# RG-LRU of a two-layer diffusion backbone: channel blocks as a pipeline skewed by one block and split by direction, without barriers, the residual kept in SBUF between post-norm and pre-norm

## Chip, cores, metric

One Trainium2 chip, 8 cores, one batch element per core (batch 8). The metric is the device time of the slowest core in microseconds (us). Cores 0 to 3 are one die, 4 to 7 the other.

Executions come in two states. In the slow one the cores of one die, or of both, show a lower granted TensorE clock and the time is some per cent longer, whatever the kernel. Ratios are the mean time of one kernel's fast runs over that of the other's of the same rounds, so not quite the ratio of the medians.

## The reference, cut to what matters

```python
D_MODEL = 2048; BATCH = 8; SEQ = 2048; CTX_LEN = 256; LRU_BLOCK = 128; D_FF = 5632; DEPTH = 2

def rglru_coeffs(v, wa, ba, wx, bx, lam):
    r = jax.nn.sigmoid(block_diag(v, wa, ba));  i = jax.nn.sigmoid(block_diag(v, wx, bx))
    log_a = -RG_C * r * jax.nn.softplus(-lam)
    return jnp.exp(log_a), jnp.sqrt(-jnp.expm1(2.0 * log_a)) * i * v

# layer 0
x   = ffn_sublayer(x, ..., w_in[0, 0], w_out[0, 0])       # pre-norm, SwiGLU, post-norm, gated residual
ctx = ffn_sublayer(ctx, ...)                              # same weights, other modulation
hx, hc = modulate(rmsnorm(x)), modulate(rmsnorm(ctx))
g, v  = jnp.split(hx @ w_in, 2, axis=-1)
v     = centred_dwconv(v)                                 # 4 taps inside each row of 64 tokens
v_ctx = centred_dwconv(hc @ w_in[:, R:])
for d, reverse in enumerate((False, True)):
    h_c  = linear_scan(*rglru_coeffs(v_ctx, ...), 0, reverse)
    y   += linear_scan(*rglru_coeffs(v, ...), h_end_of(h_c), reverse)
x = x + gate * rmsnorm((gelu(g) * y) @ rec_w_out)
x = ffn_sublayer(x, ..., w_in[0, 1], w_out[0, 1])
# layer 1: FFN, Fourier mixer, FFN.  Every shift, scale and gate is an adaLN product silu(c) @ mod_w + b
```

## The kernel before: the parts that matter

A helper records every operation with what it reads and writes, and lets the issuing engine wait for whatever is outstanding on those. A tile is tracked as a whole, not by columns:

```python
def _deps(self, stream, reads, writes):
    for r in reads:
        self._wait(stream, r.w)
    for w in writes:
        self._wait(stream, w.w)          # the last write of the same tile
        for ev in w.r:
            self._wait(stream, ev)       # its readers
```

adaLN products run in the background of the first FFN's gate/up phases; VectorE empties their PSUM:

```python
def adaln_task(l, idx, W):               # a 1 MB load, 32 matmuls of 2 columns, one evacuation
    ...
    S.op("pe", pe, reads=[rb, r_scb], writes=spair_res(k))
    S.op("dve", evac, reads=spair_res(k) + [r_vecs], writes=[r_mods[l][idx // 2]])
ada = [adaln_task(0, i, W) for i in range(32, 144, 2)]               # 56 of them
gu_phase(W, 0, 0, T0[0], stat_steps(T0[1], 0), ada[:20])             # ada[20:40], ada[40:] in the next two
```

The RG-LRU starts with the last tile's post-norm and pre-norm through memory and a barrier, and handles one block of 128 channels after the other:

```python
def rglru(carry, hx, hcb):
    for st in carry:                     # 32 post-norm and pre-norm chunks: load, compute, store, load again
        st()
    S.barrier()
    ... # weights of blocks 0 and 1, projections and convolution of block 0
    for c in range(KC):                  # 16 blocks
        ... # PE: context gates of both directions -> ACT: tanh, exp
        for d in range(2):               # PE: 8 gate matmuls, ACT: 4 tanh, 1 exp
            ...
        emit_v(c + 1)                    # PE: recurrent projection of the next block
        ... # DVE: squares; ACT: sqrt; DVE: products
        stage1(c + 1)                    # PE: gate projection; ACT: copy, gelu; DVE: convolution
        ... # DVE: four scans (context and tokens, two directions), sum, times gelu -> zs in HBM
    S.barrier()
... # zs is read back, then the output projection (mix_out), tile 0 and tile 1
```

## Time and profile before

Runs of before: 10679.41, 11927.26, 10470.75 us, and a profiled one of 10495.78 (fast). The stages below are read from the trace, as means over its 8 cores.

| stage | us |
|---|---|
| up to the end of the first FFN (three tiles, gate/up and down projections) | 2447 |
| of which gate/up of the middle tile | 572 |
| lead-in: last FFN matmul to first gate matmul of block 0 | 257 |
| 15 block periods (57.4 each) | 862 |
| tail: last block and output projection of tile 0 | 200 |
| output projection of tile 1 | 286 |
| the rest (second FFN, layer 1) | 6423 |
| all | 10476 |

The page's rows by slice of 262 us, here the DMA share (tenths) and GB/s, show why the stages have different limits:

```profile
DMA  9988878985211278986997687566555566565545
GB/s 166 155 144 162 166 143 162 180 166 139 42 30 31 51 191 170 172 157 128 166 176 142 135 169 161 118 128 125 107 133 154 152 149 122 105 131 122 122 90 140
```

The first FFN keeps the DMA engines at seven to nine tenths. In the RG-LRU, slices 11 to 14, they fall to one or two: there is room for the adaLN weights.

### The profile page before, as it was taken

What the parts mean: (1) busy time and instruction counts of PE and PEld (TensorE: products, weight loads), DVE (VectorE), ACT (ScalarE), POOL (GpSimd) and SP (SyncE); (2) the same over time, 40 slices, a digit from 0 to 9 for tenths busy, and PEclk for the clock granted to TensorE, in tenths of its full rate; (3) what the DMA queues carried; (4) which work ended last, traced back from release to release, by engine and by line L of the source; (5) the groups of instructions that cost most, each with busy time, mean ns of one, the idle gap of its engine ahead of it and who ended that gap; (6) DMA issues with size and microseconds to landing.
All of it is one profiled execution on the core that took longest, in us unless ns stands there. A gap on an engine that the chain in (4) does not pass through costs nothing.

```text
span 10494.4 us, 126561 instructions; the slowest of 8 cores (10445.1 to 10494.4 us)
## 1 busy us (share of the span) xinstructions
PE 8912.0 (85%) x47328; PEld 4369.6 (42%) x47967; DVE 2776.5 (26%) x3790; ACT 1943.4 (19%) x3068; POOL 534.5 (5%) x935
## 2 busy tenths in 40 slices
PE   3998899993567567999999999999984479999995
PEld 2655555652223223444444444444432134444442
DVE  1112211223577632121221133112224322111102
ACT  1111111122454322111111111111113221110000
POOL 0000000000000000000000000000000000000000
PEclk9999999996777688999999999999996789999997
DMA  9988878985211278986997687566555566565545
GB/s 166 155 144 162 166 143 162 180 166 139 42 30 31 51 191 170 172 157 128 166 176 142 135 169 161 118 128 125 107 133 154 152 149 122 105 131 122 122 90 140
DMA packets 541141, 1416.33 MB, mean 135 GB/s; under 512 B 65400, under 2 KB 215032, under 8 KB 489600
## 3 DMA queue, kind: packets, MB, share of 16 engines
q0 software_dynamic: 153888, 830.83, 48.1%
q1 hardware_dynamic: 386656, 577.37, 19.4%
q8 instruction: 395, 6.47, 0.3%
q14 instruction: 202, 1.65, 0.1%
HBM read 1995.21 MB, written 222.30 MB: 211 GB/s over the span
## 4 chain that ended last, share of the span: by engine, by line
PE 78%; DMA 12%; ACT 3%; DVE 3%; issue 3%; SPq 1%; DVEq 0%; ACTq 0%; POOL 0%; POOLq 0%; another core or an unknown queue 0%
PE PS L170 50%; PE PS L569 25%; DMA xl_17_67<-xT 1%; DMA xl_20_70<-xT 1%; DMA w_30_80<-modw 1%; DMA xl_20_70<-xs 1%; PE PS L325 1%; DMA xl_21_71<-xs 1%; DMA xl_19_69<-xT 1%; DMA xl_16_66<-xs 1%; PE PS L756 1%; PE PS L369 1%; PE PS L759 1%; DMA xl_15_65<-xT 0%; DMA xl_21_71<-xT 0%
## 5 line engine op out<-in xcount | busy, mean ns | idle before, releaser
L384 DVE TENSOR_TENSOR acc_12_62<-acc_12_62,sq_25_75 128x512 f32<-128x512 f32 (+1 forms) x150 | 97.8, 652 | 2027.4 <-ACT sq_25_75 L383 1955.2
L170 PE MATMUL PS<-hb_29254,w_69_29251 128*128 128x512 bf16 x2381 | 527.6, 379 | 3.4 <-ACT acc_12_62 L373 0.7
L170 PE MATMUL PS<-hb_29254,w_67_29249 128*128 128x512 bf16 x2314 | 514.5, 379 | 2.8
L170 PE MATMUL PS<-hb_29254,w_70_29252 128*128 128x512 bf16 x2119 | 474.6, 380 | 9.3 <-DMA w_70_29252<-win 6.3
L170 PE MATMUL PS<-hb_29254,w_68_29250 128*128 128x512 bf16 x2119 | 471.8, 379 | 4.3 <-DVE hid_29253 L546 1.0
L170 PE MATMUL PS<-hb_29254,w_66_29248 128*128 128x512 bf16 x2064 | 459.7, 380 | 3.2 <-issue 0.5
L170 PE MATMUL PS<-hb_82,w_28_78 128*128 128x384 bf16 x2240 | 376.4, 329 | 56.7 <-ACT hb_82 L449 36.4
L170 PE MATMUL PS<-hb_82,w_30_80 128*128 128x384 bf16 x2240 | 374.3, 328 | 20.8 <-DVE mods_2_44 L332 13.9
L170 PE MATMUL PS<-hb_82,w_29_79 128*128 128x384 bf16 x2240 | 373.4, 328 | 12.1 <-DVE mods_2_44 L332 12.0
L170 PEld LDWEIGHTS PS<-hb_29254,w_69_29251 128*128 128x128 bf16 x2432 | 236.7, 98 | 283.8 <-issue 0.6
L170 PEld LDWEIGHTS PS<-hb_29254,w_67_29249 128*128 128x128 bf16 x2368 | 230.5, 98 | 277.0 <-issue 1.8
L170 PEld LDWEIGHTS PS<-hb_29254,w_70_29252 128*128 128x128 bf16 x2176 | 212.5, 98 | 262.2 <-issue 9.7
L170 PEld LDWEIGHTS PS<-hb_29254,w_68_29250 128*128 128x128 bf16 x2176 | 212.4, 98 | 257.2 <-issue 4.7
L170 PEld LDWEIGHTS PS<-hb_29254,w_66_29248 128*128 128x128 bf16 x2112 | 206.0, 98 | 247.4 <-issue 3.4
L170 PEld LDWEIGHTS PS<-hb_82,w_28_78 128*128 128x128 bf16 x2240 | 219.3, 99 | 204.3 <-issue 64.8
L544 ACT ACTIVATE ev_23_73<-PS 128x512 f32<-128x512 f32 (+1 forms) x264 | 147.5, 559 | 834.2 <-PE PS L170 774.9
L544 ACT ACTIVATE ev_24_74<-PS 128x512 f32<-128x512 f32 (+1 forms) x266 | 148.6, 559 | 821.8 <-PE PS L170 767.7
L170 PE MATMUL PS<-hb_82,w_27_77 128*128 128x384 bf16 x1728 | 286.9, 327 | 14.1 <-DVE mods_2_44 L332 13.2
L544 ACT ACTIVATE ev_22_72<-PS 128x512 f32<-128x512 f32 (+1 forms) x262 | 145.9, 557 | 821.9 <-PE PS L170 788.1
L170 PEld LDWEIGHTS PS<-hb_82,w_30_80 128*128 128x128 bf16 x2240 | 219.4, 98 | 168.1 <-issue 26.7
L170 PEld LDWEIGHTS PS<-hb_82,w_29_79 128*128 128x128 bf16 x2240 | 219.3, 98 | 158.9 <-issue 17.1
L569 PE MATMUL PS<-hid_29253,w_67_29249 128*128 128x512 bf16 x1122 | 251.3, 381 | 5.3 <-DVE hid_29253 L546 2.1
(638 smaller groups left out, 12563.4 us busy)
## 6 DMA issues: line engine op xcount, KB each, us to landing
w_69_29251<-win POOLq DMA_DIRECT2D x38, 1024.0 KB, 13.7
w_67_29249<-win POOLq DMA_DIRECT2D x37, 1024.0 KB, 13.4
w_28_78<-win POOLq DMA_DIRECT2D x35, 1024.0 KB, 13.8
w_29_79<-win POOLq DMA_DIRECT2D x35, 1024.0 KB, 14.1
w_30_80<-win POOLq DMA_DIRECT2D x35, 1024.0 KB, 14.0
w_68_29250<-win POOLq DMA_DIRECT2D x34, 1024.0 KB, 12.1
w_70_29252<-win POOLq DMA_DIRECT2D x34, 1024.0 KB, 12.3
w_66_29248<-win POOLq DMA_DIRECT2D x33, 1024.0 KB, 12.7
```

What stands on the lines that cost most here:

```text
L170: ins = e.matmul(out, l, r, start=(i == 0), stop=(i == n - 1))
L325: ins = e.matmul(o, w, scb[:, 2 * c:2 * c + 2], start=(c == 0), stop=(c == KC - 1))
L369: ins = e.matmul(sbank(k, h, n), ones[:], acc[:, h * n:(h + 1) * n], start=True, stop=True)
L384: S.op("dve", lambda e: e.tensor_tensor(out=a, in0=a, in1=sb[:, :n], op=ALU.add), reads=[rsq], writes=[r_acc])
L544: S.op("act", lambda e, tb=tb, h=h, k=ks[0]: e.activation(out=tb[:, :n], in_=sbank(k, h, n), func=AF.Silu), reads=[rPS[2 * ks[0] + h]], wr ...
L569: ins = e.matmul(sbank(k, h, n), buf[:, (c - a) * 128:(c - a + 1) * 128], rhs(c, h), start=(c == 0), stop=(c == nk - 1))
L756: e.matmul(bank(PB, t2), gwa, vcb[:, lo + t2 * TT:lo + (t2 + 1) * TT], start=True, stop=True)
L759: ins = e.matmul(bank(PB, 2 + t2), gwx, vcb[:, lo + t2 * TT:lo + (t2 + 1) * TT], start=True, stop=True)
```

## The change

Its intent: (1) let TensorE work on the next block's projections between the gates of this one, one direction after the other, so that gates, exponentials, scans and projections overlap; (2) no barrier before or after the recurrence, and no reload of the last block; (3) keep the last tile's residual in SBUF from post-norm to pre-norm; (4) move 32 of 56 adaLN tasks from the first FFN into the idle DMA time of the recurrence.

```diff
-    ada = [adaln_task(0, i, W) for i in range(32, 144, 2)]
+    ada = [adaln_task(0, i, W) for i in range(32, 80, 2)]
-    gu_phase(W, 0, 0, T0[0], stat_steps(T0[1], 0), ada[:20])          # then [20:40], [40:]
+    gu_phase(W, 0, 0, T0[0], stat_steps(T0[1], 0), ada[:10])          # then [10:17], [17:]
-    rglru(post_steps(T0[2], 0, 1, 0, 0) + pre_steps(T0m[2], 1, 0, 1, mdst, r_mdst), hx, hcb)
+    W, posts = rglru(W, T0[2], hx, hcb, r_hxs, TS)

+    def post_resident(tl, l, s, ro, xr, r_xr, yr, slot):              # lead-in, 16 chunks of 768 columns
+        def load(m):
+            S.dma("sp", dn, ... out=yb, in_=ys[...])
+            for (off, w, src, dst, t0, which) in segs:                # 512 latent, 256 context columns
+                S.dma("sp", f"xr{m}", ... out=xr[m][:, off:off + w] ..., writes=[r_xr[m]])
+        for m in range(yr.n - 1): load(m)
+        rstd(acc, r_acc, n, slot=slot)
+        for m in range(KC):
+            ...                                                       # DVE: y * rstd, x += gate * y
+            S.op("act", ... AF.Square ...)
+            S.dma("act", f"xw{m}", ...)                               # store x, which also stays in xr[m]
+            S.op("pe", stat, ...)                                     # sum of squares
+        rstd(rsx[ro], r_rsx[ro], n, slot)

+        for b in range(3): proj(0, 0, b)                              # block 0, five banks, ahead of the above
+        for b in range(2): proj(0, 1, b)
+        post_resident(tl, 0, 0, 1, xr, r_xr, yr, 3)

+        for c in range(KC):                                           # vch, gch: chunks of block c + 1
+            g0[0](); g0[1](); hsum()                                  # hsum on POOL (sum of directions)
+            for i in range(3): take(vch); g0[2 + i]()
+            take(vch); expo(c, 0); pmul(c, 0); conv(nx, 0); msqrt(); zout(c - 1)
+            take(vch); take(vch)
+            g1[0](); take(vch); g1[1](); take(vch); g1[2](); take(gch); g1[3](); take(gch); g1[4]()
+            scan(c, 0); take(gch)
+            i0 = ada_pe(0); ada_pe(1); expo(c, 1); pmul(c, 1)         # expo(c, 1): its square on POOL
+            take(gch); conv(nx, 1); ctx_proj(nx); ctx_conv(nx); cast(nx)
+            ada_pe(2); msqrt(); take(gch); take(gch); ada_pe(3); take(gch); take(gch)
+            ada_evac(i0); scan(c, 1); gelu(nx)
... # tail: the last block's product goes straight into the matmul operand; no barrier, no reload
```

## The prediction

> **What bounds the kernel now.** I began with the page, then cut the span by the chain that ended last and asked for the busy time of each stretch. Columns: stretch, its length, then TensorE (PE), its weight loads, VectorE (DVE), ScalarE (ACT), GpSimd (POOL) busy with instruction counts; last the granted PE clock, the DMA share, GB/s.
>
> ```profile
> PEclk9999999996777688999999999999996789999997
> ...
> 203.00:684.00 481.00, 476.67 (x3431) 292.49 (x3430) 69.96 (x142) 55.91 (x124) 36.92 (x63) 1.00 0.91 148
> 920.00:1504.00 584.00, 495.11 (x3468) 298.08 (x3468) 132.29 (x237) 78.11 (x161) 37.47 (x64) 0.92 0.87 160
> 1741.00:2220.00 479.00, 476.65 (x3339) 291.12 (x3340) 112.17 (x204) 61.67 (x126) 34.56 (x60) 0.99 0.95 173
> 2456.00:2712.00 256.00, 37.77 (x151) 17.20 (x155) 98.66 (x161) 53.58 (x90) 3.75 (x6) 0.58 0.43 109
> 2712.00:3582.00 870.00, 611.18 (x2419) 261.92 (x2461) 625.52 (x418) 421.83 (x396) 16.26 (x26) 0.77 0.13 28
> 3582.00:3667.00 85.00, 7.24 (x15) 1.74 (x16) 38.25 (x21) 19.20 (x17) 2.65 (x5) 0.50 0.42 98
> 3667.00:3773.00 106.00, 105.26 (x475) 47.73 (x485) 18.01 (x26) 29.35 (x57) 7.49 (x15) 0.99 0.77 174
> 3773.00:4063.00 290.00, 138.52 (x575) 59.55 (x583) 122.89 (x162) 82.91 (x139) 10.07 (x18) 0.74 0.79 194
> ```
>
> The first three rows are the gate/up phases of the three tiles of the first FFN; the middle one is 103 us longer, at about the same PE work. 2456 to 2712 is the lead-in of the RG-LRU: last post-norm, last pre-norm, barrier, block 0's projections; PE works 38 of 256 us. 2712 to 3582 is 15 steady blocks of 58.0 us, where no engine is full: PE 41 us, DVE 42, ACT 28 each. After 3582 comes the last block with a barrier and a reload of z (85 us), then the output projection of tile 0 (106) and of tile 1 (290, held by transfers).
>
> Two lists of waits name the holders, for PE from 920 to 1220 and from 2456 to 2712 (total, times, longest):
>
> ```profile
> PE PS L170 <- DVE mods_2_44 L332: 52.9, 5, 13.9
> ...
> PE PS L369 <- DVE rsx_14_64 L384: 133.5, 1, 133.5
> PE PS L170 <- DMA wi_35_24157<-recin: 77.4, 1, 77.4
> ```
>
> Line 332 empties an adaLN product out of PSUM. It sits on DVE behind post-norm steps that wait for x loads, and PE runs out of PSUM slots. Then 133.5 us is PE waiting while 32 small post-norm chunks go through memory; the 77.4 us that look like a weight load are really the pre-norm chunks ahead of the barrier.
>
> These rows from the whole kernel and from one block's time order (start, us) price the operations:
>
> ```profile
> L806 DVE TENSOR_TENSOR_SCAN bH_49_24171<-bC_47_24169,cH_24186,bB_45_24167 128x2048 f32<-128x2048 f32 x16 | 71.7, 4484 | 1.7
> L775 DVE TENSOR_TENSOR bH_48_24170<-bC_46_24168 128x2048 f32<-128x2048 f32 x16 | 36.7, 2292 | 114.5 <-ACT bC_46_24168 L769 114.5
> L763 ACT ACTIVATE bA_24165<-PS,hgb_24187 128x1024 f32<-128x1024 f32 x64 | 71.3, 1114 | 96.2 <-PE PS L759 96.2
> ...
> 2963.34 15.77 PE L170 MATMUL PS<-hx_20830,wi_36_24158 128*128 128x512 bf16 x63
> 2967.76 1.28 ACT L778 ACT_TABLE_LOAD   x1
> 2969.47 1.99 ACT L780 ACTIVATE bH_48_24170<-bH_48_24170,oneb_51 128x2048 f32<-128x2048 f32 x1
> 2981.24 13.97 PE L170 MATMUL PS<-hx_20830,wi_36_24158 128*128 128x512 bf16 x63 [2.13 <-ACT vp_24162 L693]
> ```
>
> A warm 512-column matmul costs 14/64 = 0.219 us start to start, so eight (half a bank) cost 1.75.
>
> **The Trainium skill.** (1) "GPSIMD Engine Reference", Elementwise side-by-side cycle accounting: a 2048-column fp32 two-input op takes 4497 ns on GpSimd, 2293 on VectorE. The 2292 above agrees; GpSimd computes nothing in this trace, so I scale: 5.1 us for 2304 columns, an estimate. (2) "SBUF — State Buffer", Who interferes with whom: a VectorE op with two SBUF inputs and a GpSimd op that reads SBUF exclude each other. No run yet shows it. (3) "ScalarE: Activation LUTs", What ACT_TABLE_LOAD costs: 1283 ns plus a drain of about 1380. The trace agrees with the load and shows no drain: load at 2967.76, next activation at 2969.05. (4) "TensorE: Matmul & The Clock Gate", Part 1: an idle window of about 3.4 us halves the clock. The two 63-matmul runs agree: 15.77 after the thinly used gate stage, 13.97 after a 2.1 us gap, so 1.8 us a cold start.
>
> **Part 1, adaLN moved out of the first FFN.** 32 of its 56 double tasks go to the RG-LRU as 64 single ones; the three phases keep 10, 7, 7 of 20, 20, 16. One task is 0.78 us of PE (chain) and a 1 MB load. Tiles 0 and 2, full of PE, save 10 and 9 tasks: 8 + 7 us. Tile 1 saves 13 x 0.78 = 10 us and most of its 584 - 495 = 89 us idle, because 13 of the 64 weight-sized loads go and line 332 with them: I take 80. Sum 105.
>
> **Part 2, lead-in.** Post-norm now runs on 16 chunks of 768 columns with six loads ahead, x stays in SBUF, squares are summed by PE, and pre-norm rereads nothing. PE does five banks of projections meanwhile (80 x 0.219 = 17.5 us, hidden). Loads 16 x 2 x 393 KB = 12.6 MB, stores 6.3 MB; at the 194 to 200 GB/s of the output stretch, 95 us for all. Allow 90 until the last chunk; square sum, square root and the 5.0 us reciprocal 10; pre-norm 16 x 1 us (ACT: 0.56 + 0.42) 16; remaining projections, convolution and casts 16. Sum 132 against 256: saves 124.
>
> **Part 3, the block.** Context and tokens become one 2304-column scan per direction, convolutions read PSUM, one square and the sum of directions go to GpSimd. Work per block: PE 128 x 0.219 + gates 4 + context 1.9 + adaLN 1.6 = 35.5; DVE: conv 7.6, context 1.6, casts 1.7, two products of 2.56 per direction 10.2, scans 10.1, output 2.3 = 33.5; ACT: tanh 10.8, exp 6.9, sqrt 4.4, identity 2.5, gelu 2.2, five table loads 6.4 = 33. Nobody alone would take 36, but the gates share one PSUM pair (banks 6, 7) while PE runs in order. Walk from PE's last projection chunk at 0: gelu of its half 1.4; table load and two context tanh 3.6; four gate tanh, each one chunk plus two gate matmuls (2.2) apart, end at 12.2; two exp 16.8; identity, table load and sqrt 21.3; table load and context tanh 23.6. PE ran out at 18.1, waiting for that tanh to free bank 6. From there: gates to 30.8, then chunk, adaLN, chunk, context projection, adaLN, four chunks: 44.9. I add 2 for the third adaLN weight, whose buffer is refilled only after the first is used (half of the 8.2 us of a 1 MB block load), and 2 for a cold start. Period 49, saving 15 x 9 = 135. DVE ends its second scan at about 51, which overlaps the next block's gates.
>
> **Part 4, tail.** No barrier; the last block ends at about 55 (GpSimd sum after the last scan, direct product into the matmul operand) with three output columns accumulated up to 14/16 in the shadow; then 13 x 32 x 0.219 + 3 = 94. 149 against 85 + 106 = 191, less 5 for evacuation: saves 38. Tile 1's projection keeps its small chunks and its 50 MB (six streams of 8.4) at 194 GB/s: still about 290.
>
> Sum 105 + 124 + 135 + 38 = 402. The fast executions of before are 10471 and 10496, mean 10483; so 10080 in the fast state. The other two, 10679 and 11927, are slower in a way that I put down to the chip's slow state.
>
> **Rivals.** (a) *The recurrence stays bound by the ACT–PE ping-pong through banks 6 and 7.* With cold starts at both stalls, slow GpSimd and a sixth table load the period is 54 and the loop saves 60: total about 325, 10160. For it: the clock of 0.77 in the loop, and that all engines need 33 to 36. Against: seven chunks fill the gate gaps, as nothing did before. (b) *The true pipeline works* and the period is 41 to 43: saves 240, total 505, 9980. It would need ACT to get through exp, sqrt and two loads before PE runs out; the walk says 5 us late. (c) *The lead-in is hidden badly*: if small-row transfers give only 110 GB/s, as 2456 to 2712 averaged, its loads and stores take 170 and it saves 40. Against: that stretch is latency with two or three loads ahead, not bandwidth. (d) *The DMA relief of tile 1 does not come*, because 66 norm steps in 42 ticks still wait for loads: saves 40 instead of 90. All of a, c and d at their worst still leave about 190 us, just under 2%.
>
> **Range and chances.** Independent errors of 40 (loop), 30 (lead-in), 30 (FFN), 15 (tail) give about 60; 8 in 10 is 80 on the fast side, widened upwards for the slow state: 9980 to 10220. The 2% line is 10275: faster 0.90, same 0.09, slower 0.01.
>
> **What would show it.** Right: the middle gate/up phase under 510 us with PE full; under 150 us from the end of the first FFN to the first tanh; block period 47 to 52 with one PE gap of 5 to 7 us in front of the second direction's gates, put down to ACT; GpSimd products of about 5 us; no gap for z at the end. Wrong: a period over 55 or under 43; DVE products stretched to 5 us or more beside GpSimd's (the port); later phases longer because the output projection's transfers moved.

## The result, and the profile after

The changed kernel's four timed runs were 10169.65 and 10143.57 (fast), 11012.23 and 11619.86 (slow): median 10590.94. A fifth run took 10156.6 (fast). The trace read below is that of the run of 10169.65. Those of before, in the same rounds, were 10470.75 and 10464.84 (fast), 10679.41 and 11927.26: median 10575.08. The medians mix states and say nothing of the change. The ratio of the fast runs is 0.9703, with a 95% interval of 0.9672 to 0.9733: 3.0% faster.

Stages, in us, mean of the 8 cores of each profiled run; the lower rows are the experiments, told below (e3_store_late and e9_best: only the four cores of the undisturbed die). The metric, the time of the slowest core, moves less in places: the means of the fast runs are 10156.6 for the changed kernel and 10138.9, 10206.2, 10153.4 (one run), 10111.0, 10069.9, 10126.2, 10033.8, 10028.8 and 9991.1 (one run) for e1 to e9. Fast runs of one kernel differ by up to 27 us, so effects smaller than that are read from the stages and not from the totals.

| kernel | first FFN | of it middle gate/up | lead-in | 15 blocks | period | tail | tile 1 | rest | all |
|---|---|---|---|---|---|---|---|---|---|
| before | 2447 | 572.5 | 256.9 | 861.6 | 57.4 | 200.3 | 286.0 | 6423 | 10476 |
| changed | 2359 | 506.2 | 148.8 | 769.2 | 51.3 | 156.5 | 285.5 | 6429 | 10148 |
| difference | -88 | -66 | -108 | -92 | -6.1 | -44 | 0 | +5 | -328 |
| predicted | -105 | -90 | -124 | -135 | -9 | -38 | 0 | 0 | -402 |
| e1_ada_late | 2365 | 509.0 | 147.0 | 720.5 | 48.0 | 157.3 | 286.8 | 6426 | 10102 |
| e2_ada_back | 2461 | 580.0 | 147.6 | 713.8 | 47.6 | 151.6 | 286.7 | 6421 | 10183 |
| e3_store_late | 2359 | 504.4 | 131.7 | 768.8 | 51.3 | 156.7 | 289.4 | 6413 | 10118 |
| e4_chunks_early | 2364 | 510.8 | 148.6 | 697.5 | 46.5 | 159.7 | 289.4 | 6422 | 10081 |
| e5_both | 2364 | 509.4 | 130.7 | 697.2 | 46.5 | 158.8 | 286.3 | 6417 | 10054 |
| e6_one_wait | 2362 | 506.9 | 116.5 | 767.4 | 51.2 | 157.6 | 287.6 | 6416 | 10107 |
| e7_lead | 2361 | 506.7 | 98.1 | 697.2 | 46.5 | 159.4 | 286.5 | 6418 | 10020 |
| e9_best | 2328 | 471.6 | 100.8 | 681.4 | 45.4 | 161.0 | 287.9 | 6426 | 9985 |

The page of the changed kernel, granted clock by slice, answers to the first line that the prediction shows:

```profile
PEclk9999999997898879999999999999977799999997
```

The hollow of the clock around the recurrence is shorter and less deep. The stretches, with the same columns as in the prediction: three gate/up phases, lead-in, 15 blocks, tail, tile 1.

```profile
200.60:670.90 470.30, 468.88 (x3108) 284.20 (x3108) 67.64 (x129) 57.07 (x125) 29.22 (x52) 0.99 0.73 129
911.50:1417.60 506.10, 476.35 (x3055) 285.89 (x3054) 132.58 (x226) 77.74 (x163) 28.10 (x51) 0.97 0.84 156
1658.00:2126.00 468.00, 465.20 (x3010) 281.17 (x3008) 110.10 (x190) 59.79 (x125) 27.07 (x50) 1.00 0.85 155
2360.30:2511.40 151.10, 45.81 (x186) 17.73 (x184) 70.14 (x84) 44.58 (x63) 2.11 (x4) 0.62 0.56 143
2511.40:3281.00 769.60, 597.97 (x3418) 272.55 (x3417) 489.82 (x316) 494.67 (x405) 172.50 (x118) 0.90 0.38 72
```

TensorE is busy for 598 of 770 us in the blocks, 78% instead of 70%, and the granted clock there rises from 0.77 to 0.90. The middle gate/up phase still has about 30 us without TensorE work. The list of TensorE's waits in it (who waited, for what, total, times, longest) names the same holder as before, smaller:

```profile
PE PS L178 <- DVE mods_2_44 L356: 22.7, 2, 11.8
```

Line 356 is line 332 of before, the evacuation of an adaLN product: 55.6 us in 6 waits became 22.7 in 2.

Lines of one block in the order of time (start, us, engine, line; in brackets the idle time before it and what ended it). The prediction's walk puts its zero at the end of the last projection chunk, here 2974.3:

```profile
2983.73 1.12 ACT L855 ACTIVATE gB_47_21849<-PS,hgb_56 128x1024 f32<-128x1024 f32 x1 [1.04 <-PE PS L851]
...
2990.78 1.19 ACT L778 ACTIVATE vcA_21845<-PS,vecs_43 128x1024 f32<-128x1024 f32 x1
2991.99 1.28 ACT L882 ACT_TABLE_LOAD   x1
2993.28 2.22 ACT L882 ACTIVATE gM_21851<-gM_21851,qtb_57 128x2304 f32<-128x2304 f32 x1
...
2997.80 1.01 PE L851 MATMUL PS<-vcb_21846,gwr_42_21844 128*128 128x512 bf16 x2 [6.73 <-ACT gB_48_21850 L838]
2998.60 3.62 PE L766 MATMUL PS<-hx_19546,wi_39_21841 128*128 128x512 bf16 x8
...
3011.14 4.04 POOL L878 TENSOR_TENSOR gM_21851<-gA_46_21848 128x2304 f32<-128x2304 f32 x1
3015.26 1.28 ACT L882 ACT_TABLE_LOAD   x1 [1.04 <-POOL gM_21851 L878]
3015.52 0.54 PE L178 MATMUL PS<-scb_52,wa_55_21857 128*128 128x2 bf16 x16 [1.97 <-DMA wa_55_21857<-modw]
3016.01 5.46 PE L766 MATMUL PS<-hx_19546,wi_39_21841 128*128 128x512 bf16 x16
```

The square root ends at 2995.50, which is 21.2 after zero (the walk says 21.3), and TensorE goes on at 23.5 (23.6), after the predicted gap, here 6.73 us, put down to ACT. The eight matmuls behind it take 3.62 us instead of the 1.89 of the others: the predicted cold start. What the walk did not have is the last line: after a wait of only 1.97 us for an adaLN weight, 16 matmuls take 5.46 us where two warm groups take 3.78. That is a second cold start (a stretch of half clock), 1.7 us in this block. The clock granted in the four stretches of this period (last three columns: clock, DMA share, GB/s):

```profile
2995.86:3002.69 6.83, 4.89 (x12) 1.75 (x13) 6.73 (x4) 2.89 (x4) 0.00 (x0) 0.50 0.19 77
3002.69:3016.34 13.65, 11.53 (x103) 6.57 (x102) 9.84 (x6) 8.29 (x7) 5.13 (x3) 1.00 0.38 70
3016.34:3019.75 3.41, 3.26 (x9) 0.90 (x7) 2.76 (x6) 3.38 (x3) 0.59 (x1) 0.50 0.69 107
3019.75:3047.06 27.31, 20.30 (x108) 8.99 (x106) 13.80 (x7) 18.45 (x16) 6.11 (x4) 1.00 0.40 73
```

In the 15 block periods each core has 29 or 30 such stretches at 0.50, two in a block.

### The profile page after: what moved, and what is told of

The parts are those of the page before. It is cut to its first block, busy times and chain, and to the rows that moved or that the text cites. A ratio compares the mean times of both kernels' runs of the same rounds, so it can differ in the third digit from the quotient of the medians.

```text
span 10168.3 us, 127066 instructions; the slowest of 8 cores (10128.1 to 10168.3 us)
## 1 busy us (share of the span) xinstructions
PE 8902.2 (88%) x47995; PEld 4352.2 (43%) x47995; DVE 2602.3 (26%) x3573; ACT 2016.4 (20%) x3052; POOL 678.7 (7%) x999
## 4 chain that ended last, share of the span: by engine, by line
PE 82%; DMA 10%; ACT 2%; DVE 2%; issue 2%; SPq 1%; DVEq 0%; ACTq 0%; POOL 0%; POOLq 0%
PE PS L178 49%; PE PS L593 25%; PE PS L766 4%; PE PS L987 2%; DMA w_34_88<-modw 1%; DMA xl_22_76<-xs 1%; DMA wa_55_21857<-modw 1%; PE PS L851 1%; PE PS L349 1%; PE PS L393 1%; DMA xl_19_73<-xs 0%; DMA xl_22_76<-ys 0%; DMA xl_22_76<-xT 0%; DMA xl_24_78<-xT 0%; ACT gM_21851 L882 0%
## 5 line engine op out<-in xcount | busy, mean ns | idle before, releaser
L178 PE MATMUL PS<-hb_90,w_34_88 128*128 128x384 bf16 x2176 | 363.7, 329 | 11.1 <-DVE mods_2_44 L356 10.9
L178 PEld LDWEIGHTS PS<-hb_28966,w_90_28963 128*128 128x128 bf16 x2432 | 237.0, 98 | 285.0 <-issue 2.7
L178 PEld LDWEIGHTS PS<-hb_28966,w_88_28961 128*128 128x128 bf16 x2368 | 230.5, 98 | 276.6 <-issue 1.2
L178 PEld LDWEIGHTS PS<-hb_28966,w_91_28964 128*128 128x128 bf16 x2176 | 212.4, 98 | 258.8 <-issue 5.8
L178 PEld LDWEIGHTS PS<-hb_28966,w_89_28962 128*128 128x128 bf16 x2176 | 212.2, 98 | 255.9 <-issue 2.9
L178 PEld LDWEIGHTS PS<-hb_28966,w_87_28960 128*128 128x128 bf16 x2112 | 205.4, 98 | 245.7 <-issue 0.3
L178 PEld LDWEIGHTS PS<-hb_90,w_34_88 128*128 128x128 bf16 x2176 | 213.9, 98 | 154.4 <-issue 16.3
L178 PEld LDWEIGHTS PS<-hb_90,w_32_86 128*128 128x128 bf16 x2048 | 201.1, 98 | 181.6 <-issue 51.7
L178 PEld LDWEIGHTS PS<-hb_90,w_33_87 128*128 128x128 bf16 x2176 | 213.6, 98 | 143.5 <-issue 5.1
```

The costliest lines, as they stand in the source:

```text
L178: ins = e.matmul(out, l, r, start=(i == 0), stop=(i == n - 1))
```

## The experiments

All kernels below gave correct results. e1 to e4 ran in one call on one chip, e5 to e8 in a second on another, e9 in a third. The fast runs of before beside them were 10508.13; 10486.14 and 10609.65; 10464.37 and 10492.47.

### e1_ada_late: the third adaLN product two chunks later

```diff
-            ada_pe(2)
             msqrt()
             take(gch)
             take(gch)
+            ada_pe(2)
             ada_pe(3)
```

> The changed kernel with one move: in each block the third adaLN product goes from in front of four projection chunks to behind two of them, beside the fourth. Theory: its weight lands 2.0 us after PE asks for it, and the gap also drops the PE clock, so that 16 matmuls behind it take 5.5 us instead of 3.6. With the wait gone the block period falls from 51.2 to about 47.3, and the kernel by 15 x 3.9 = 58 us, ratio to before about 0.965. Rival: another engine's tail (gelu of the second half on ACT, or the casts on DVE) is as late as PE, so the wait was free: period 50 or more, total within 15 us of the changed kernel.

Measured: period 48.0 (47.3 was expected), fast runs 10143.16 and 10134.63; the mean over cores is 46 us under the changed kernel's, the mean of the fast runs 18. TensorE's waits in the same 245 us of the recurrence (2720 to 2965, core 1), first the changed kernel, then e1_ada_late:

```profile
PE PS L851 <- ACT gB_48_21850 L838: 33.6, 5, 6.7
PE PS L851 <- ACT gB_47_21849 L838: 9.4, 5, 1.9
PE PS L178 <- DMA wa_55_21857<-modw: 9.1, 5, 1.9
```

```profile
PE PS L851 <- ACT gB L838: 49.7, 11, 6.7
...
PE PS L178 <- DMA wa<-modw: 0.3, 1, 0.3
```

The wait for the weight is gone from the list, and 3.3 us of the period went with it, which is more than the wait's 1.9. The rest goes with the clock that the wait cost: on six of the eight cores the 15 periods now hold 15 stretches at half clock instead of 30. The predicted term "2 for the third adaLN weight" was right as a wait, and wrong as a cost.

### e2_ada_back: all adaLN tasks back in the first FFN

```diff
-    ada = [adaln_task(0, i, W) for i in range(32, 80, 2)]     # + all ada_pe and wa_load of the recurrence
+    ada = [adaln_task(0, i, W) for i in range(32, 144, 2)]
-    ... ada[:10] ... ada[10:17] ... ada[17:]
+    ... ada[:20] ... ada[20:40] ... ada[40:]
```

> The changed kernel with all 56 adaLN tasks back in the first FFN (20, 20, 16) and none in the RG-LRU. Theory: the first FFN goes back to 481, 584 and 479 us (plus 90 in all), and the block loses four adaLN products (2.4), the 2.0 us wait and one cold start (1.9), period about 45, which gives back 15 x 6.2 = 93 us: total within 25 us of the changed kernel, so that moving adaLN was worth about nothing as it was placed. Rival 1: the long middle phase came from the norm steps and not from the weights, then the first FFN stays near 508 in the middle and the total falls by 80. Rival 2: the adaLN products cost the loop nothing, period stays 50 to 51, total grows by 90.

Measured: fast runs 10199.13, 10196.05 and 10223.51. The first FFN grows by 102 us (8, 74 and 20 in the three gate/up phases), the blocks give back 55 and the tail 5; the total is 35 us above the changed kernel. So both rivals fall, and so does the theory, which had the move worth about nothing: it pays, about 100 us where it was taken away and about 60 charged where it was put. (The third phase is 10 us longer than in before; why was not looked into.) The period is 47.6, not 45. It is only 0.4 us under e1_ada_late's, where the work is still there and the wait is not, so the wait and its cold start could be nearly all of that charge. This is not shown: e2_ada_back still has two stretches at half clock in a block (28 or 29 in 15 blocks), the second now at the next block's first gates. The middle phase's list of waits returns to that of before (55.6, 6, 13.9):

```profile
PE PS L178 <- DVE mods L356: 57.2, 6, 14.4
```

### e3_store_late: x stored only after all post-norm chunks

```diff
-            S.dma("act", f"xw{m}", ...)            # in each chunk
+        def stores(): ...                          # 16 stores from the SP queue, after the last chunk
```

> The changed kernel with the 6.3 MB of x stores of the lead-in issued after the last post-norm chunk, from SBUF, instead of after each chunk. Theory: the lead-in is bound by transfer bandwidth (12.6 MB of loads and 6.3 of stores in 110 us), so the last square sum comes about 35 us earlier (at 72 to 80 us after the end of the FFN) and the stores pass beside the first block; lead-in 150 to about 118, total minus 30. Rival: the loads' own latency with six ahead sets the pace, or the stores delay block 0, whose tiles lie on x: then less than 10 us is gained.

Measured: the profiled run was slow on cores 0 to 3, so cores 4 to 7 are read; one fast run, 10153.36. The lead-in is 17 us shorter, half of what the theory said, and the one fast run is no faster than the changed kernel's (10156.6); the last square sum comes 90 us after the FFN's end instead of 110. The stretch of the loads, and the one in which the SP queue then issues the stores (from 2450 on, so beside the last chunks), core 5:

```profile
2366.00:2447.00 81.00, 29.34 (x111) 10.08 (x108) 37.76 (x49) 17.22 (x23) 1.05 (x2) 0.64 0.57 167
2447.00:2475.00 28.00, 1.60 (x4) 0.27 (x4) 20.22 (x20) 13.37 (x21) 0.00 (x0) 0.50 0.79 248
```

With nothing but loads, the DMA engines were busy 57% of the time at 167 GB/s. So the loads were not held by bandwidth, which my theory had taken for granted; something else paced them.

### e4_chunks_early: four projection chunks before the second direction's gates

```diff
             g1[0]()
-            take(vch)
-            g1[1]()
-            ...
+            take(vch); take(vch); take(gch); take(gch); take(gch)
+            g1[1](); take(gch); g1[2](); take(gch); g1[3](); take(gch); g1[4]()
             ...                                      # and the third adaLN product late, as in e1
```

> Four projection chunks moved in front of the second direction's gates, where PE idles 6.7 us for ACT, and the adaLN products late as in e1_ada_late. Theory (PE and ACT alternate through banks 6 and 7): the idle is filled, the tail after the last gate is short, and the period becomes what ACT and DVE need from last tanh to next tanh, 45 to 46; total minus 80 against the changed kernel, 25 below e1_ada_late. Rival: the 10 us that DVE needs after the last tanh (product, convolution, context, casts) then hold the next block's gates, and the period stays at 47 or more, no better than e1_ada_late.

Measured: period 46.5, half a us over the theory and under the rival's 47; fast runs 10101.34 and 10120.75; the mean over cores is 67 us under the changed kernel's. The gap moves to the next block's first gates: there TensorE waits for the last tanh of the context, behind the gelu, the square root and GpSimd's product. Two lines of its time order, core 7:

```profile
2955.84 1.28 ACT L882 ACT_TABLE_LOAD   x1 [1.93 <-POOL gM L878]
2963.57 1.01 PE L851 MATMUL PS<-vcb,gwr 128*128 128x512 bf16 x2 [4.09 <-ACT gB L838]
```

So TensorE was fed, and still meets ScalarE's chain through the block, now at another place. That this chain sets the period is only a reading here; e9_best puts it to a test.

### e5_both: e3 and e4 together

```diff
+ both edits above
```

> Stores after the chunks (as in e3_store_late) and four chunks ahead of the second direction's gates with the third adaLN product late (as in e4_chunks_early), together. They act in different stages, so the gains should add: lead-in 132 us (from the first FFN's last matmul to the first gate matmul), block period 46.5, sum 17 + 72 less what moves elsewhere, so fast runs of about 10085 (e4_chunks_early had 10101 and 10121). Rival: the stores' 21 us of transfers run into block 0's weight and adaLN loads, block 0 to 2 get longer and the gain of the stores is lost: 10100 or more, with the first periods above 49.

Measured: fast runs 10064.17, 10067.55 and 10077.9; lead-in 130.7, period 46.5. The gains add, and a little better than expected; the late stores disturb no block.

### e6_one_wait: the changed kernel, with the two x loads of a chunk issued together

```diff
-            for (off, w, src, dst, t0, which) in segs:
-                S.dma("sp", f"xr{m}", lambda e, ...: e.dma_start(out=xr[m][:, off:off + w], ...), writes=[r_xr[m]])
+            S.dma("sp", f"xr{m}", lambda e: [e.dma_start(out=xr[m][:, off:off + w], ...)
+                                             for (off, w, ...) in segs], ..., writes=[r_xr[m]])
```

The reason came from the SP queue's own list of waits in the changed kernel's lead-in. The three longest for an x load; there are 16 such lines, one for each chunk, down to 3.5 us, 80 us in all (the 87 in the expectation is a mis-sum):

```profile
SPq L96 <- DMA xr_57_21859<-xT: 10.3, 1, 10.3
...
SPq L96 <- DMA xr_62_21864<-xT: 7.2, 1, 7.2
SPq L96 <- DMA xr_66_21868<-xT: 5.5, 1, 5.5
```

The queue waits until the 512 latent columns have landed before it issues the load of the 256 context columns, because both write the tile `xr[m]` and a tile is tracked as a whole. The Trainium skill, "DMA: Bandwidth & Descriptors", section "Anatomy of one DMA — SWDGE (gpsimd) path", says that any semaphore wait happens on the issuing sequencer before dispatch. It says so of loads that GpSimd issues; these are SP's, and their 16 waits in this trace agree, and every later load in that queue stands behind them.

> The changed kernel with one edit: the two loads of one x chunk (512 latent columns and 256 context columns) are issued together. In the changed kernel both write one tile, which is tracked as a whole, so the queue lets the second wait until the first has landed: its own list of waits shows 16 such waits, 3.5 to 10.3 us long, about 87 us in all, inside the 110 us that the 16 chunks take. Theory: these waits set the pace of the chunks. Without them the last square sum comes when 18.9 MB have moved at the 296 GB/s that the late stores reached (64 us) or when VectorE has done its 16 x 2.4 us after the 5 us reciprocal (about 65 us), so at 65 to 80 instead of 110, lead-in 105 to 118 instead of 149, fast runs about 35 us under the changed kernel's, 10110 to 10130. Rival 1: bandwidth sets the pace (18.9 MB at the 168 to 203 GB/s seen in the changed kernel): last square sum at 95 or later, lead-in 134 or more. Rival 2: the loads come earlier but the stores, which the ScalarE queue issues, now hold ScalarE: its squares wait, last square sum at 90 to 100.

Measured: fast runs 10115.53 and 10136.77, lead-in 116.5. The last square sum comes at 75.8 us. The same work, from the FFN's end to the last square sum, in the changed kernel and in e6_one_wait (last three columns: clock, DMA share, GB/s):

```profile
2361.10:2471.50 110.40, 31.37 (x117) 10.58 (x114) 41.11 (x54) 19.17 (x25) 1.05 (x2) 0.61 0.71 185
```

```profile
2371.00:2446.80 75.80, 31.33 (x117) 10.60 (x114) 40.69 (x54) 19.14 (x25) 1.06 (x2) 0.65 0.91 270
```

The same 20 MB (75.8 us at 270 GB/s, 110.4 at 185) moved half as fast again, and no wait for an x load is left in that list. Both rivals fall in the form in which they were put: what set the pace was first of all a wait between two loads. The stores cost too, as e3_store_late has shown, but less.

### e7_lead: e5, loads together, and the square sum ahead of the projections

```diff
+ e5_both, and the loads of e6_one_wait
-        for b in range(3): proj(0, 0, b)
-        for b in range(2): proj(0, 1, b)
         ...
         rstd(acc, r_acc, n, slot=slot)
+        ahead()                                    # the five banks of projections
```

> e5_both with the x loads of a chunk issued together, and the last tile's square-sum matmuls ahead of the five banks of projections (in the changed kernel they stand behind them on TensorE, and ScalarE waits 15 us for them before the first chunk can start). Theory: with neither a wait between loads nor stores in the way, only VectorE paces the chunks: reciprocal done at about 12 us after the FFN's end instead of 27, 16 x 2.4 = 39, last square sum at 51 to 60, then 39 us as before to the first gate matmul: lead-in 90 to 100 against 132 of e5_both, so 30 to 40 us faster than it, about 10050. Rival: the loads alone (12.6 MB) do not exceed 200 GB/s, the last one lands at 63 us or later, lead-in 105 to 112.

Measured: fast runs 10036.94 and 10030.58, lead-in 98.1. From the FFN's end to the last square sum it takes 59.0 us, inside what was expected:

```profile
2360.30:2419.30 59.00, 31.85 (x116) 11.11 (x116) 40.41 (x54) 19.14 (x25) 1.06 (x2) 0.71 0.98 285
```

The DMA engines are at 0.98, which looks like a limit, but is not yet what holds the chunks: VectorE works on them almost without a break, from 2375.2 to 2417.3, and in these 59 us waits only 6.8 for loads. The share holds the stores too, which the SP queue issues from 2405 on. So the theory, that VectorE paces the chunks, stands, and its rival falls: from 2380 to 2405, before the first store, the engines moved 316 GB/s. The waits, the stores and the projections together had cost 51 us (110.4 - 59.0).

### e8_sq_act: the second direction's square as an exponential on ScalarE

```diff
-            if d == 0:
-                S.op("act", ... out=gM, in_=gA[d], func=AF.Exp, scale=c2, bias=c2 ...)
+            S.op("act", ... out=gM, in_=gA[d], func=AF.Exp, scale=c2, bias=c2 ...)      # both directions
-            if d == 1:
-                S.op("pool", ... out=gM, in0=gA[d], in1=gA[d], op=ALU.mult ...)
```

> e7_lead with the second direction's square taken on ScalarE as an exponential with doubled coefficients (2.3 us) instead of GpSimd's product (4.0 us). In e4_chunks_early ScalarE waited 1.9 us (3.1 in other blocks) for that product ahead of the square root, and TensorE waited 3.9 to 4.1 us for the gelu and tanh behind it at the next block's first gates. Theory: that chain sets the period, so it shortens by 4.0 - 2.3 = 1.7 us, perhaps 2.2 with the hand-over: period 44.3 to 45.0, 22 to 33 us in 15 blocks. Rival: TensorE's own work or VectorE's scan takes over at once: period 46 or more, and the waiting of TensorE only moves.

Measured: fast runs 10032.71 and 10024.98, against 10036.94 and 10030.58 of e7_lead: no difference that counts. The profiled run was slow, but cores 0, 1, 6 and 7 became slow only after the recurrence (their first gate/up phases took 470 us): on these the period is 46.5, lead-in 98.4. The theory falls, and by its own numbers. ScalarE's time order, core 1, in e7_lead and then in e8_sq_act, from the exponential to the square root's table load:

```profile
2866.17 2.30 ACT L880 ACTIVATE gA<-gA,coef 128x2304 f32<-128x2304 f32 x1
2872.91 1.28 ACT L887 ACT_TABLE_LOAD   x1 [2.83 <-POOL gM L883]
```

```profile
2958.71 2.30 ACT L877 ACTIVATE gM<-gA,coef 128x2304 f32<-128x2304 f32 x1
2964.97 1.28 ACT L883 ACT_TABLE_LOAD   x1
```

From 2866.17 to 2872.91 are 6.7 us, from 2958.71 to 2964.97 6.3. The 4.0 us of GpSimd's product already lay beside 1.8 us of ScalarE's own work, so ScalarE only waited for 1.9 to 2.8 us of it, and the second exponential costs 2.3. Up to the end of the next block's context tanh the chain takes 14.1 us, against 14.2. I had subtracted durations (4.0 - 2.3) where I should have subtracted the wait.

### e9_best: no adaLN task in the middle phase, the square on VectorE

```diff
-    gu_phase(..., ada[:10])  ...  gu_phase(..., ada[10:17])  ...  gu_phase(..., ada[17:])
+    gu_phase(..., ada[:14])  ...  gu_phase(..., [])          ...  gu_phase(..., ada[14:])
-            S.op("pool", ... out=gM, in0=gA[d], in1=gA[d], op=ALU.mult ...)
+            S.op("dve", ... out=gM, in0=gA[1], in1=gA[1], op=ALU.mult ...)              # after pmul(c, 1)
```

> e7_lead with two edits in different stages. (1) The first FFN's middle gate/up phase gets no adaLN tasks (14, 0 and 10 instead of 10, 7 and 7). In the changed kernel that phase still takes 506 us instead of 470, and TensorE waits there 22.7 us for line 356, which empties an adaLN product out of PSUM on VectorE behind post-norm steps. Theory: that is the rest of the same hold-up, so the phase falls to 474 to 482, and the other two gain 3 tasks of about 0.8 us each: net 20 to 28 us. Rival: the post-norm loads hold the phase, adaLN or not: 495 or more. (2) The second direction's square is taken on VectorE (2.56 us, after the product with the convolution) instead of on GpSimd (4.04 us). e8_sq_act left the period at 46.5 because its second exponential of 2.3 us takes ScalarE's own time, where it only waited 1.9 us for GpSimd: so the chain from the last tanh to the next block's gates stayed 14 us. VectorE's product ends about 1.4 us sooner and costs ScalarE nothing. Theory: period 45.0 to 45.4. Rival: VectorE's convolution and cast, 2.6 us later, become what the next gates wait for: period 46.5 or more. Together, if both theories hold, about 45 us faster than e7_lead's 10031 to 10037.

Measured: one fast run, 9991.05 (seven others were slow), against 10464.37 and 10492.47 of before: 0.953. On the undisturbed die the middle phase is 471.6 (theory 474 to 482; a little better) and the period 45.4 (45.0 to 45.4); both theories hold. In the middle phase all of TensorE's waits together are now one line:

```profile
PE PS L393 <- DVE rsx L408: 4.3, 1, 4.3
```

That the post-norm loads were the holder, as the rival says, is excluded: they are all still there. Seven adaLN loads of 1 MB went together with the evacuations, and no run takes away one without the other; but the DMA share of the phase hardly moved (0.84 in the changed kernel, 0.82 here), so the evacuations are the likelier cause. On core 1 ScalarE's chain from the exponential to the next block's context tanh takes 13.1 us instead of e7_lead's 14.2, which is the 1.1 us of the period (but see the steps of the period under "Not settled").

The traces of this run also show what the prediction had named as a hazard: VectorE's product beside GpSimd's sum of directions, core 1:

```profile
2885.34 4.51 POOL L901 TENSOR_TENSOR gH<-gH,gB 128x2048 f32<-128x2048 f32 x1 [7.10 <-DVE gB L895]
2888.03 4.24 DVE L870 SCALAR_TENSOR_TENSOR gB<-gB,vcA 128x2304 f32<-128x2304 f32 x1 [2.85 <-ACT gB L860]
```

The product takes 2.56 us when it is alone. Here it takes 4.24 and ends 2.42 us after the sum. So it is in all 60 overlaps on the four undisturbed cores: 2.75 to 4.62 us long, and always ended 2.41 or 2.42 us after the sum. The two exclude each other, as point (2) of the prediction's list from the skill says; the sum, which had started first, is not slowed.

e9_best is the best version tried: 4.7% under before, against 3.0% of the changed kernel.

## Why the prediction was right or wrong

**The direction, the mechanism and the place of the gap** were right: all four parts gained, tile 1 kept its 286 us as it said ("still about 290"), and the walk through the block met two of its times within 0.1 us: the end of the square root (21.2, said 21.3) and TensorE's going on (23.5, said 23.6). That is partly luck. It has a table load ahead of the first context tanh that does not come, so these end at 2.0 instead of 3.6, and leaves one out ahead of the two exponentials, so they end at 16.6 instead of 16.8: the errors nearly cancel. And TensorE ran out at 16.8 instead of 18.1, which makes the gap 6.7 us instead of 5.5. The fast runs, 10144 to 10170, lie within its range, 60 to 90 us above its 10080.

**The range.** The step that failed is "widened upwards for the slow state". Of the four timed runs of each kernel two were slow; those of the changed kernel were 8.6% and 14.6% over its lowest. The median over all runs, 10591, is therefore a mean of a fast and a slow run and lies far above 10220. The prediction says which state its figure is for; it then let an upper side of 140 us stand for the other, where before's own 11927 already showed 1457 over its lowest. A range for all runs needed both states with their chances, or the sentence that it holds for fast runs alone.

**Part 1, 105 predicted, 88 measured.** Tiles 0 and 2 gave 8.7 and 10.3 us for the 8 and 7. The term "I take 80" of tile 1's idle time was too high by about the 24 us in which 66 came short of 90: seven tasks were left in that phase, and two evacuations still stood behind post-norm on VectorE, 22.7 us. e9_best takes those seven away and the phase falls by 35 us, to what tiles 0 and 2 need. Fewer tasks of a harmful kind are not as good as none; and rival (d), which blames the norm steps' loads, is excluded. The prediction's words "line 332 with them" are the step that failed: with seven of 20 tasks left, that line was still there.

**Part 2, 124 predicted, 108 measured.** The failed step is "at the 194 to 200 GB/s of the output stretch, 95 us for all. Allow 90 until the last chunk". It took 110.4. The rate of another stretch was taken for the rate of the transfers, and it is not: e6_one_wait moved the same bytes at 270 GB/s, and e7_lead's stretch ran at 285. What paced the chunks were 16 waits of the queue between two loads of one tile, about 80 us in all. They were in the code: two loads with the same `writes`. The stores between the chunks cost some 17 us more (e3_store_late). A second hold-up was overlooked: "PE does five banks of projections meanwhile (... hidden)" puts them ahead of the square-sum matmuls that the first chunk needs, and ScalarE waits 15 us for these. How much of the 15 us this cost by itself no run shows, because e7_lead changes other things too. The terms after the last chunk, 10, 16 and 16, came to 6, 21 and 13 on core 7: a sum of 40 against 42.

**Part 3, 135 predicted, 92 measured; period 51.3 instead of 49.** The mis-sized term is "2 for the third adaLN weight". The wait is 1.97 us, but TensorE's clock falls again, which costs 1.7 us more. The prediction had counted one fall of the clock, at the long gap, and its point (4) speaks of idle windows of about 3.4 us, which this wait does not reach. e1_ada_late removes both and the period falls to 48.0. The other error is on the side of before: "15 x 9" takes 58.0 for every period, while the first and last were 55.3 and 51.1 on core 2, so the mean is 57.4 and 8 of the 135 us did not exist. GpSimd's square, estimated at 5.1 us from a sum of two tensors, takes 4.04, and ScalarE waits 1.04 us for it. Rival (a), ping-pong through one PSUM pair, names the right shape but the wrong size; rival (b), 41 to 43, was not reached by any edit. A reading of why: once TensorE is fed, ScalarE's chain of exponential, two table loads, square root, gelu and tanh holds it at 46.5 (e4_chunks_early), and e9_best, which shortens this chain by 1.1 us, gets 45.4.

**Part 4, 38 predicted, 44 measured.** Right, though its own terms give 37 (191 - 149 - 5). The gap for z is gone, and TensorE's longest waits in the last block are now 11.1 us for ScalarE ahead of the second direction's gates, and 8.1 and 2.3 us for adaLN weights ahead of the output projection.

**Not settled.** Why the clock falls at one wait of 2 us and not at others is left open. The changed kernel's period is 51.3, and 49 plus the 1.7 of the second cold start is 50.7. The other 0.6 us may belong to something: in every recurrence traced here, all stretches of the clock record (those of 0.50 and of 1.00, as in the table of the block above) are whole multiples of the shortest, 3.413 us, and the steady period (blocks 6 to 14) is a whole number of these steps or of thirds of them. It is 58.03 us in before (17.0 steps), 51.2 in the changed kernel (15.0) and 47.8 in both e1_ada_late and e2_ada_back on most cores (14.0). In e4_chunks_early, e5_both, e7_lead and e8_sq_act three blocks together take about 41 steps (140 us), and in e9_best about 40 (on core 1 44.8, 46.3 and 45.4 us in turn). So a saving inside a block may be rounded up or down: the near equality of e1 and e2, and e7 and e8 with the same period, could come from this as well as from the costs named above, and the 1.1 us of e9_best is a third of a step. No run separates the two; that ScalarE's chain alone sets the period is therefore likely, not shown.

The other hazard named, VectorE's products "stretched to 5 us or more beside GpSimd's", did not come in the changed kernel, because there they never overlap GpSimd's work: they take 2.56 us. It is real all the same: in e9_best they do overlap, and take up to 4.62. The convolution's steps, which read one of their tensors from PSUM, took 1.27 us beside GpSimd's square as without it.

## What to carry to other kernels

A rate taken from another stretch is not a bandwidth: before it is used, look at the queue's own waits and ask whether the loads ahead of a pipeline can really be in flight together; two loads into one tracked tile cannot. Price an operation that moves to another engine by the wait it removes on the path, not by its duration, and a short wait of TensorE by its length plus the slower matmuls behind it. When the longest wait is gone, look again before naming the next holder: a DMA share of 0.98 was not it here. Where background work harms because one engine empties its results in order behind slow steps, move all of it out of that phase, not most.

## What the Trainium skill lacked or had wrong

- "ScalarE: Activation LUTs", What ACT_TABLE_LOAD costs: about 1380 ns of drain are stated for every switch. In the recurrence the load takes 1.28 us and no drain is seen on either side: in the block shown above the activation before it ends at 2991.97, the load starts at 2991.99, and the square root at 2993.28.
- "TensorE: Matmul & The Clock Gate", Part 1: an idle window of about 3.4 us is stated. Here a wait of 1.97 us, between context matmuls of 256 columns and adaLN matmuls of 2, was enough: the clock was 0.50 for the next 3.41 us and 16 matmuls took 5.46 us instead of 3.78. The same page tells further on that short idles between groups of matmuls can make the clock oscillate, but gives no length for them.
- No page tells that a loop with a fall of the clock in every pass settles on a period of whole clock steps: 17.0, 15.0 and 14.0 steps of 3.413 us here. Whether the steps cause it is open.
- "GPSIMD Engine Reference", Elementwise side-by-side cycle accounting: 4497 ns for an addition of two tensors of 2048 columns agrees (4.52 us for the sum of directions). A product that reads one tensor twice is not covered: 2304 columns took 4.04 us, 1.75 ns a column instead of 2.2. Whether the operation or the single tensor makes the difference is not shown.
